# A one-core transformer block: half banks of a set in another order, matmuls of 512 columns in pieces with 8 products, outputs of the plain part issued by SyncE

## The chip, the core and the metric

The kernel runs on one core of a Trainium2 chip. The core has TensorE (PE, matrix products into PSUM), VectorE (DVE), ScalarE (ACT), GpSimd (POOL) and SyncE (SP, which here only issues transfers). The metric is the time of the device for one execution in microseconds; less is better. The engines run side by side, each through its own list of instructions in order, and wait for each other on semaphores.

## The reference

One residual block in float32: model width 2048, sequence 512, batch 1.

```python
hn = rmsnorm(h, norm_mix_g)
proj = hn @ w_in + b_in                       # 2048 x 10248
(q, k, v, o_pre, i_pre, f_pre, cb, cc, ch, gm_pre, gc_pre) = jnp.split(proj, offs, axis=-1)
hm = mlstm_chunkwise(...)                     # 4 heads, chunks of 64
y_m = (head_norm(hm) * jax.nn.sigmoid(o_pre)) @ w_branch_m
y_c = (cb * causal_dwconv(cc * ch, conv_w)) @ w_branch_c
merged = jax.nn.sigmoid(gm_pre) * y_m + jax.nn.sigmoid(gc_pre) * y_c
h = h + merged @ w_out
hn = rmsnorm(h, norm_ffn_g)
u = causal_dwconv(hn @ w_up, ffn_conv_w, ffn_conv_b)   # 2 x 5504 channels
gate, val = jnp.split(u, 2, axis=-1)
h = h + (jax.nn.silu(gate) * val) @ w_down
return rmsnorm(h, norm_out_g)
```

Nearly all the arithmetic is in the dense products with w_in, w_branch, w_out, w_up and w_down.

## The kernel before

Activations lie with channels on the 128 partitions and the 512 time steps along the free axis. The dense products are done by a scheme of the Strassen and Winograd kind: a 2 x 2 arrangement of blocks takes 7 block products and some sums of weights and of activations instead of 8 products. Each float32 factor is split into a high and a low part, and each product is the sum of three matmuls: high weights by high activations (L281), high weights by low activations (L282), low weights by high activations (L283). The helper `three` issues these three.

**Items, pieces, halves.** An item makes two pairs of output blocks. It runs through `nq` pieces of its contraction, each of two halves; `cell_mm` issues one half. An ordinary half has 7 products, so 21 matmuls of 256 columns. One piece of some items (`it.eight`) does the plain 8 products, without the sums of weights (`eight_task`); its halves have 24 matmuls of 256 columns. There are 24 such pieces. Their high weights come from ScalarE at L186 and L187, the others' at L233.

**PSUM.** There are 8 banks of 512 float32 columns, each a tile of its own. Items use two sets in turn: set 0 is banks 0, 1, 2, set 1 is banks 4, 5, 6. A set has six half banks of 256 columns. `PRODUCTS` says which weights and activations go into which bank and half. Bank 3 (`P_BANK`) takes the first product of both sets, a half each; bank 7 (`SIDE`) serves norms and the mLSTM part.

**Evacuation.** After the last half of an item, ScalarE copies the product in bank 3 (`evac_first`, L305), and VectorE adds the banks up in four instructions (`evac_ops`, L311 to L314): L311 reads the first bank of the set, L312 and L313 the second, L314 the third. They stand on VectorE among the sums of weights (L218, L223) and the low weights of the next piece (L237, or L191 and L192 in eight pieces). The low weights have three buffers; PE waits for them at L283, and VectorE waits at L237 for a buffer that PE has freed.

**Plain part.** The last rows of w_down are done without the scheme. There are 16 blocks, `lasts`, of 18 matmuls each (`last_mm`, L1202 to L1204), numbered n = 0 to 15; n below 8 is the first half of the time steps. Block n goes into bank 0, 1, 2 or 4 by n mod 4 (`LBANKS`). Then follow, one step of the program later, the sum with the residual on VectorE (`last_post`, L1215), its square on ScalarE (L1216) and the sum of squares on VectorE (`last_acc`, L1220). After block 9 a matmul with a constant matrix (`last_sum`, L1225, into bank 5; for the second half bank 6) gives the mean over the channels of the first half; `last_root` makes the reciprocal root of it (L1232 on ScalarE, for which a table has to be loaded, then L1233 to L1235 on VectorE). `last_scale` multiplies a block by that and issues its output (L1254). Some blocks have been multiplied by the gain on ScalarE ahead of that (`last_gain`, L1241) and need one instruction on VectorE (L1248); the others need two (L1252).

**Order and waits.** The order of instructions on each engine is the order in which the program issues them, written out by hand in the loop over steps, with a credit for VectorE's time that decides when the stores and sums behind an item (`posts`) go out. Waits are put in for each tile by what was last written or read in it: an instruction that touches a tile waits for the last other engine's access to the tile as a whole.

These lines decide what the change touches:

```python
PRODUCTS = [(1, 0, 0, 0), (6, 4, 0, 1), (5, 3, 1, 0), (4, 2, 1, 1), (2, 1, 2, 0), (3, 6, 2, 1)]
bank = [psum.tile([P, T], F32, tag=f"bank{i}", name=f"bank{i}") for i in range(8)]
P_BANK, SIDE = bank[3], bank[7]
SETS = (bank[0:3], bank[4:7])
LBANKS = (bank[0], bank[1], bank[2], bank[4])
LCOLS = (bank[5], bank[6])
```

## Time and profile before

| | us |
|---|---|
| median of 3 runs | 2601.21 |
| lowest and highest of them | 2599.85, 2602.29 |
| the profiled execution | 2603.19 |
| its span | 2601.5 |

The profiled execution is 1.98 us above the median. Its span is what the rows of the trace are measured in: it starts with the first instruction and ends with the last, and 1.7 us lie outside of it. The main part, items and pieces, runs to 2545.7 us, the plain part from there to the end. PE is busy for 98% of the span, and the granted clock of PE is full in nearly all of the 40 slices; VectorE is busy for 82%, ScalarE for 51%, GpSimd for 33%. A row of a timeline has the start, the duration, the engine, the line, what is written and read (by tile name), partitions and columns, and in brackets how long the engine idled before it and what ended that. Matmul rows overlap: one of 256 columns lasts 0.28 us from issue to end, while the next starts 0.12 us after it. So the pitch of starts is what counts for a stream.

### The profile page before, as it was taken

The page shows a single profiled execution, that of the slowest core. Times are in us where ns is not written, and L with a number is a line of the kernel's source. Part 1 is how long each engine was busy: PE and PEld are TensorE (multiplying, and loading weights), DVE is VectorE, ACT ScalarE, POOL GpSimd, SP SyncE. Part 2 cuts the span into 40 slices and gives each one's busy share as a digit, 9 for nine tenths or more (in the row PEclk, how much of TensorE's full clock was granted, in tenths as well). Part 3 has the DMA queues.
Part 4 walks back from the last instruction along what each step waited for, and adds up shares of the span by engine and source line. Part 5 has one row for each costly group of instructions (what it writes and reads, how often), then busy time and mean ns, then how long its engine had stood idle before and what let it go on. Part 6 is the DMA issues. An engine that isn't in the chain of part 4 may idle for free.

```text
span 2601.5 us, 55134 instructions
## 1 busy us (share of the span) xinstructions
PE 2548.2 (98%) x20886; PEld 2528.9 (97%) x20886; DVE 2123.1 (82%) x3239; ACT 1316.3 (51%) x1731; POOL 862.5 (33%) x996
## 2 busy tenths in 40 slices
PE   9999999999999999999899999999999999999997
PEld 8999999999999999999899999999999999999997
DVE  8687778886777888967889888888888898879766
ACT  7454554546556544445554544454444554545444
POOL 3343333333333212232333333333333323353430
PEclk9999999999999999999999999999999999999998
DMA  9799889898998899999989988898989889999995
GB/s 256 176 238 241 234 225 253 221 256 217 231 253 221 233 297 235 267 271 245 234 220 227 224 224 218 222 224 223 223 221 224 223 223 234 249 273 252 270 228 169
DMA packets 479003, 609.83 MB, mean 234 GB/s; under 512 B 44640, under 2 KB 309856, under 8 KB 478736
## 3 DMA queue, kind: packets, MB, share of 16 engines
q1 hardware_dynamic: 307280, 423.46, 51.5%
q0 software_dynamic: 144224, 137.67, 35.2%
q10 hardware_dynamic: 27232, 45.17, 4.8%
q8 instruction: 163, 2.67, 0.4%
q14 instruction: 104, 0.85, 0.1%
HBM read 541.65 MB, written 60.82 MB: 232 GB/s over the span
## 4 chain that ended last, share of the span: by engine, by line
PE 65%; DVE 5%; DMA 3%; issue 2%; ACT 0%; POOL 0%; DVEq 0%; SPq 0%; ACTq 0%; POOLq 0%
PE bank L283 21%; PE bank L282 21%; PE bank L281 21%; DVE act L361 1%; DVE wl L237 1%; DMA raw<-in_w_out_dram 1%; DMA raw<-in_w_up_dram 1%; DVE raw L218 0%; DMA xraw<-mc_d 0%; DMA xraw<-a_d 0%; DVE xraw L344 0%; PE bank L639 0%; DMA mc_d<-z 0%; PE bank L1204 0%; PE bank L1203 0%
## 5 line engine op out<-in xcount | busy, mean ns | idle before, releaser
L283 PE MATMUL bank<-act,wl 128*128 128x256 f32 x6712 | 1906.1, 284 | 24.3 <-DVE wl L237 23.7
L281 PE MATMUL bank<-act,wh 128*128 128x256 f32 x6712 | 1914.0, 285 | 4.9 <-ACT z L305 2.1
L282 PE MATMUL bank<-act,wh 128*128 128x256 f32 x6712 | 1903.2, 284 | 2.1 <-DVE act L361 2.1
L233 ACT ACTIVATE wh<-raw 128x896 fp32r<-128x896 f32 x904 | 858.2, 953 | 1076.1 <-PE bank L282 719.0
L283 PEld LDWEIGHTS bank<-act,wl 128*128 128x128 f32 x6712 | 1292.2, 193 | 29.2 <-DVE wl L237 29.1
L281 PEld LDWEIGHTS bank<-act,wh 128*128 128x128 f32 x6712 | 1292.2, 193 | 8.5 <-DVE z L311 2.4
L282 PEld LDWEIGHTS bank<-act,wh 128*128 128x128 f32 x6712 | 1292.2, 193 | 5.4 <-DVE act L361 2.5
L237 DVE TENSOR_TENSOR wl<-raw,wh 128x896 fp32r<-128x896 f32 x904 | 982.7, 1088 | 372.2 <-PE bank L283 244.2
L255 POOL DMA_DIRECT2D raw<-in_w_up_dram x344 | 299.2, 952 | 578.7 <-DMA raw<-in_w_up_dram 243.8
L255 POOL DMA_DIRECT2D raw<-in_w_dram x284 | 247.1, 944 | 505.2 <-DMA raw<-in_w_dram 320.9
L255 POOL DMA_DIRECT2D raw<-in_w_down_dram x160 | 141.5, 1002 | 253.0 <-DMA raw<-in_w_down_dram 144.2
L218 DVE TENSOR_TENSOR raw<-raw 128x256 f32<-128x256 f32 x452 | 189.8, 420 | 11.4 <-DMA raw<-in_w_up_dram 5.1
L223 DVE TENSOR_TENSOR raw<-raw 128x256 f32<-128x256 f32 x452 | 189.6, 420 | 0.3
L358 ACT ACTIVATE act<-xraw 128x1792 fp32r<-128x1792 f32 (+1 forms) x52 | 86.9, 1672 | 63.1 <-DVE xraw L354 61.1
L361 DVE TENSOR_TENSOR act<-xraw,act 128x1792 fp32r<-128x1792 f32 (+1 forms) x52 | 103.4, 1988 | 0.0
L688 DVE TENSOR_TENSOR z<-z,rstd 128x1024 f32<-128x1024 f32 x83 | 101.1, 1219 | 0.0
L311 DVE TENSOR_TENSOR z<-bank,z 128x512 f32<-128x512 f32 x122 | 83.6, 685 | 16.2 <-ACT z L305 12.6
L312 DVE TENSOR_TENSOR z<-bank,z 128x512 f32<-128x512 f32 x122 | 83.5, 684 | 0.8
L314 DVE TENSOR_TENSOR z<-bank,z 128x512 f32<-128x512 f32 x122 | 83.4, 684 | 0.0
L255 POOL DMA_DIRECT2D raw<-in_w_out_dram x48 | 42.9, 1019 | 105.3 <-DMA raw<-in_w_out_dram 41.2
L255 POOL DMA_DIRECT2D raw<-in_w_v_dram x32 | 38.6, 1360 | 52.1 <-DMA raw<-in_w_v_dram 32.8
L313 DVE TENSOR_TENSOR z<-bank,z 128x256 f32<-128x256 f32 x122 | 51.8, 424 | 4.2
(247 smaller groups left out, 1302.5 us busy)
## 6 DMA issues: line engine op xcount, KB each, us to landing
raw<-in_w_up_dram SPq DMA_DIRECT2D x172, 512.0 KB, 5.8
raw<-in_w_dram SPq DMA_DIRECT2D x144, 512.0 KB, 6.0
raw<-in_w_up_dram SPq DMA_DIRECT2D x344, 128.0 KB, 4.0
raw<-in_w_up_dram POOLq DMA_DIRECT2D x344, 128.0 KB, 5.5
raw<-in_w_down_dram SPq DMA_DIRECT2D x80, 512.0 KB, 6.6
raw<-in_w_dram SPq DMA_DIRECT2D x284, 128.0 KB, 4.2
raw<-in_w_dram POOLq DMA_DIRECT2D x284, 128.0 KB, 5.3
raw<-in_w_down_dram SPq DMA_DIRECT2D x160, 128.0 KB, 4.5
```

Of the source, the lines that this page charges most:

```text
L218: V.tensor_add(x[:, 6], x[:, 5], x[:, 0])
L223: V.tensor_add(x[:, 2], x[:, 6], x[:, 1])
L233: A.activation(seven(t.wh[r]), half(r), AF.Copy)
L237: V.tensor_sub(seven(t.wl[r]), half(r), seven(f(t.wh[r])))
L255: G.dma_start(at(i), a21, accum_op=ALU.add)
L281: PE.matmul(ps, h, xh, start=start, stop=False, skip_group_check=True)
L282: PE.matmul(ps, h, xl, start=False, stop=False, skip_group_check=True)
L283: PE.matmul(ps, l, xh, start=False, stop=stop, skip_group_check=True)
L311: return [lambda: V.tensor_add(z[:, 0:4:3], b0, two(z[:, 1])), lambda: V.tensor_add(z[:, 1:3], b1, two(z[:, 3])), lambda: V.tensor_add(z[: ...
L358: A.activation(t.act[:, :m], t.raw[:, :m], AF.Copy)
L361: V.tensor_sub(t.act[:, NW:NW + m], t.raw[:, :m], f(t.act[:, :m]))
L688: V.tensor_mul(sb_pair(it.z), sb_pair(it.z), two(rstd))
```

## The change

The three banks of a set become one PSUM tile of 1536 columns, and the six half banks get new products, so that in a piece with 8 products the two half banks that share weights lie side by side and their activations can be read with one stride. Two `three`s of 512 columns replace four of 256. The evacuation reads the same products at their new places. `bank` stays as a list of views of the set tiles, so that the gates and the plain part use the same columns as before, but as parts of the set tiles. In the plain part, outputs are issued by SyncE instead of ScalarE; the gain is multiplied ahead for blocks 1, 3, 5 and 8 to 15, at other places than before, instead of blocks 4 to 15; and one small activation, issued in the step of block 6, uses the table of the root. Lines behind the middle of the file move by one: L1215 is L1216 afterwards, L314 is L315.

```diff
@@ -38,7 +38,7 @@
 K_LAST = 40
 
 
-PRODUCTS = [(1, 0, 0, 0), (6, 4, 0, 1), (5, 3, 1, 0), (4, 2, 1, 1), (2, 1, 2, 0), (3, 6, 2, 1)]
+PRODUCTS = [(1, 0, 0), (6, 4, 2), (5, 3, 3), (4, 2, 4), (2, 1, 1), (3, 6, 5)]
 P1 = (0, 5)
 
 
@@ -120,9 +120,9 @@
     def fwc(which, j): return col(152 + 2 * NF * which, j)
     def fw_neg(which, j): return pneg[:, 24 + NF * which + j:24 + NF * which + j + 1]
 
-    bank = [psum.tile([P, T], F32, tag=f"bank{i}", name=f"bank{i}") for i in range(8)]
-    P_BANK, SIDE = bank[3], bank[7]
-    SETS = (bank[0:3], bank[4:7])
+    SETS = [psum.tile([P, 3 * T], F32, tag=f"set{i}", name=f"set{i}") for i in range(2)]
+    P_BANK, SIDE = (psum.tile([P, T], F32, tag=s, name=s) for s in ("pbank", "side"))
+    bank = [SETS[i // 4][:, i % 4 * T:(i % 4 + 1) * T] if i % 4 < 3 else (P_BANK, SIDE)[i // 4] for i in range(8)]
 
     mA, mB, mC = C([P, 1280], F32, "mA"), C([P, 1032], F32, "mB"), C([P, T], F32, "mC")
     z2 = C([P, 2 * T], F32, "z2")
@@ -277,16 +277,17 @@
 
         def three(ps, ws, xs, start, stop=last):
             h, l = (w[r][:, ws * P:(ws + 1) * P] for w in (t.wh, t.wl))
-            xh, xl = (x[:, b + xs * SW:b + xs * SW + SW] for b in (0, NW))
+            xh, xl = (x[:, b:b + NW].rearrange("p (s n) -> p s n", n=SW)[:, xs] for b in (0, NW))
             PE.matmul(ps, h, xh, start=start, stop=False, skip_group_check=True)
             PE.matmul(ps, h, xl, start=False, stop=False, skip_group_check=True)
             PE.matmul(ps, l, xh, start=False, stop=stop, skip_group_check=True)
 
         if q == it.eight:
             assert not first
+            halves_ = slots(SETS[it.set])
             for k in range(2):
-                for ws, xs, b, half in ((k, 2 * k, 0, 0), (k, 2 * k + 1, 2, 0), (2 + k, 2 * k + 1, 1, 1), (2 + k, 4 + k, 2, 1)):
-                    three(SETS[it.set][b][:, half * H2:(half + 1) * H2], ws, xs, False, last and k == 1)
+                three(halves_[:, 0:2], k, slice(2 * k, 2 * k + 2), False, last and k == 1)
+                three(halves_[:, 4:6], 2 + k, slice(2 * k + 1, 5 + k, 3 - k), False, last and k == 1)
             t.wh[r] = t.wl[r] = None
             return
 
@@ -295,8 +296,8 @@
 
         if last:
             p1()
-        for ws, xs, b, half in PRODUCTS:
-            three(SETS[it.set][b][:, half * H2:(half + 1) * H2], ws, xs, first and half == 0)
+        for ws, xs, i in PRODUCTS:
+            three(slots(SETS[it.set])[:, i], ws, xs, first and i in (0, 2, 4))
         if not last:
             p1()
         t.wh[r] = t.wl[r] = None
@@ -307,11 +308,11 @@
     def evac_ops(it):
 
         z = slots(it.z)
-        b0, b1, b2 = (slots(b) for b in SETS[it.set])
-        return [lambda: V.tensor_add(z[:, 0:4:3], b0, two(z[:, 1])),
-                lambda: V.tensor_add(z[:, 1:3], b1, two(z[:, 3])),
-                lambda: V.tensor_add(z[:, 3], b1[:, 0], z[:, 2]),
-                lambda: V.tensor_add(z[:, 1:3], b2, z[:, 1:3])]
+        b = slots(SETS[it.set])
+        return [lambda: V.tensor_add(z[:, 0:4:3], b[:, 0:4:2], two(z[:, 1])),
+                lambda: V.tensor_add(z[:, 1:3], b[:, 3:5], two(z[:, 3])),
+                lambda: V.tensor_add(z[:, 3], b[:, 3], z[:, 2]),
+                lambda: V.tensor_add(z[:, 1:3], b[:, 1:6:4], z[:, 1:3])]
 
 
     def cell_task(xs, c, d, scale=None, key=None, eight=False):
@@ -464,7 +465,7 @@
 
     combos = [(cs, ct) for cs in range(4) for ct in range(cs, 4)]
     ccol, ecol = C([P, 12, 4], F32, "ccol"), C([P, 4, 4], F32, "ecol")
-    GATE, GATE1 = SETS[1][2], SETS[1][1][:, :H2]
+    GATE, GATE1 = bank[6], bank[5][:, :H2]
     gb = [mA[:, :T], mA[:, T:2 * T], mB[:, :T], mB[:, T:2 * T], mC, z2[:, :T], z2[:, T:]]
 
     gst = mC[:, :KD * 8].rearrange("p (k n) -> p k n", n=8)
@@ -1251,7 +1252,7 @@
                 s = h[:, b * H2:(b + 1) * H2]
                 V.scalar_tensor_tensor(s, s, g_out(j), row, op0=ALU.mult, op1=ALU.mult)
         j1, j2 = kpair(p)
-        A.dma_start(outT[j1:j2 + 1:j2 - j1, :, half * H2:(half + 1) * H2].rearrange("j p t -> p j t"),
+        SP.dma_start(outT[j1:j2 + 1:j2 - j1, :, half * H2:(half + 1) * H2].rearrange("j p t -> p j t"),
                      h.rearrange("p (j t) -> p j t", j=2))
 
 
@@ -1501,11 +1502,10 @@
             for _ in range(2 if it.n < 12 else 1):
                 if finals:
                     last_scale(0, finals.popleft())
-        if not main and it.n > 7:
-            if it.n < 12:
-                last_gain(lasts[it.n - 4])
-            if it.n > 9:
-                last_gain(lasts[it.n - 2])
+        if not main and (it.n in (3, 5, 7) or it.n > 9):
+            last_gain(lasts[it.n - 2])
+        if not main and it.n == 6:
+            A.activation(sm("ny")[:, :1], eps, AF.Abs_reciprocal_sqrt)
     l, = lq
     while lsum:
         last_acc(lsum.pop())
```

**PE, a half of an eight piece.** The rows are the first 12 of 24 matmuls of such a half before (wh and wl are high and low weights, act the activations), and then the first 6 of 12 of the same half afterwards.

```order
L281 MATMUL bank0_80<-act_827_10589,wh_836_10665 128x256 [waits Activation_49]
L282 MATMUL bank0_80<-act_827_10589,wh_836_10665 128x256
L283 MATMUL bank0_80<-act_827_10589,wl_842_10726 128x256 [waits DVE_49]
L281 MATMUL bank2_82<-act_827_10589,wh_836_10665 128x256
L282 MATMUL bank2_82<-act_827_10589,wh_836_10665 128x256
L283 MATMUL bank2_82<-act_827_10589,wl_842_10726 128x256
L281 MATMUL bank1_81<-act_827_10589,wh_836_10665 128x256 [waits Activation_49]
L282 MATMUL bank1_81<-act_827_10589,wh_836_10665 128x256
L283 MATMUL bank1_81<-act_827_10589,wl_842_10726 128x256 [waits DVE_49]
L281 MATMUL bank2_82<-act_827_10589,wh_836_10665 128x256
L282 MATMUL bank2_82<-act_827_10589,wh_836_10665 128x256
L283 MATMUL bank2_82<-act_827_10589,wl_842_10726 128x256
```

```order
L281 MATMUL set0_80<-act_827_10585,wh_836_10661 128x512 [waits Activation_49]
L282 MATMUL set0_80<-act_827_10585,wh_836_10661 128x512
L283 MATMUL set0_80<-act_827_10585,wl_842_10722 128x512 [waits DVE_49]
L281 MATMUL set0_80<-act_827_10585,wh_836_10661 128x512 [waits Activation_49]
L282 MATMUL set0_80<-act_827_10585,wh_836_10661 128x512
L283 MATMUL set0_80<-act_827_10585,wl_842_10722 128x512 [waits DVE_49]
```

Each pair of `three`s that used the same columns of weights has become one with 512 columns, and all write one tile, set0.

**PE, plain part, from block 4 to block 5.** The last three matmuls of block 4 and the first three of block 5, before and then afterwards. act_2472 is the tile of the activations, act_2498 that of the weights, high and low.

```order
L1202 MATMUL bank0_80<-act_2472_30241,act_2498_30574 128x256
L1203 MATMUL bank0_80<-act_2472_30241,act_2498_30574 128x256
L1204 MATMUL bank0_80<-act_2472_30241,act_2498_30574 128x256
L1202 MATMUL bank1_81<-act_2472_30241,act_2498_30574 128x256 [waits Activation_49]
L1203 MATMUL bank1_81<-act_2472_30241,act_2498_30574 128x256
L1204 MATMUL bank1_81<-act_2472_30241,act_2498_30574 128x256 [waits DVE_49]
```

```order
L1203 MATMUL set0_80<-act_2472_29661,act_2498_29994 128x256
L1204 MATMUL set0_80<-act_2472_29661,act_2498_29994 128x256
L1205 MATMUL set0_80<-act_2472_29661,act_2498_29994 128x256
L1203 MATMUL set0_80<-act_2472_29661,act_2498_29994 128x256 [waits DVE_49,Activation_49]
L1204 MATMUL set0_80<-act_2472_29661,act_2498_29994 128x256
L1205 MATMUL set0_80<-act_2472_29661,act_2498_29994 128x256
```

Before, block 5 began in another bank than block 4's, and its first wait was for ScalarE, for the weights. Now it writes the tile that block 4 has written, and its first matmul also waits for VectorE: for the sum L1216 of block 4, which reads that tile.

**ScalarE, plain part, around the first root.** L1216 (L1217 afterwards) is the square of a block, L1241 (L1242) the gain, L1232 (L1233) the root, L1508 the new small activation; hf are the residual tiles. The rows before begin with the gain of block 4 and the square of block 8, those afterwards with the square of block 5.

```order
L1241 ACTIVATE hf_2496_30520<-hf_2496_30520,pcol_71 128x256 [waits Activation_49]
L1241 ACTIVATE hf_2496_30520<-hf_2496_30520,pcol_71 128x256
L1216 ACTIVATE mB_89<-hf_2500_30627 128x512 [waits DMAHW3_49,DVE_49]
L1232 ACT_TABLE_LOAD [waits PE_49]
L1232 ACTIVATE rstd_79<-bank5_85,rs1_106 128x256 [waits Pool_49]
L1241 ACTIVATE hf_2496_30520<-hf_2496_30520,pcol_71 128x256 [waits Activation_49]
L1241 ACTIVATE hf_2496_30520<-hf_2496_30520,pcol_71 128x256
L1216 ACTIVATE mB_89<-hf_2500_30627 128x512 [waits DMAHW4_49,DVE_49]
L1254 DMA out_0_dram<-hf_2496_30520 128x2x256 [waits DVE_49] x2
```

```order
L1217 ACTIVATE mB_85<-hf_2496_29940 128x512 [waits DMAHW0_49,DVE_49]
L1508 ACT_TABLE_LOAD
L1508 ACTIVATE ny_147<-rs1_102 128x1 [waits Pool_49]
L1217 ACTIVATE z1_89<-hf_2496_29940 128x512 [waits DMAHW1_49,DVE_49]
L1242 ACTIVATE hf_2496_29940<-hf_2496_29940,pcol_71 128x256 [waits Activation_49]
L1242 ACTIVATE hf_2496_29940<-hf_2496_29940,pcol_71 128x256
L1217 ACTIVATE z0_88<-hf_2500_30049 128x512 [waits DMAHW2_49,DVE_49]
L1217 ACTIVATE mB_85<-hf_2500_30049 128x512 [waits DMAHW3_49,DVE_49]
L1233 ACTIVATE rstd_79<-set1_81,rs1_102 128x256 [waits PE_49]
L1217 ACTIVATE mB_85<-hf_2500_30049 128x512 [waits DMAHW4_49,DVE_49]
L1242 ACTIVATE hf_2500_30049<-hf_2500_30049,pcol_71 128x256 [waits Activation_49]
```

The load of the table, which before waited for the matmuls of L1225, stands three squares ahead of the root now and waits for nothing. The root itself waits for PE. The outputs have left ScalarE's list.

## The prediction

> **What bounds the kernel now.** I read the page first: busy time, then the chain that ended last, then the groups.

> ```profile
> span 2601.5 us, 55134 instructions
> PE 2548.2 (98%) x20886; PEld 2528.9 (97%) x20886; DVE 2123.1 (82%) x3239; ACT 1316.3 (51%) x1731; POOL 862.5 (33%) x996
> PE 65%; DVE 5%; DMA 3%; issue 2%; ACT 0%; POOL 0%; DVEq 0%; SPq 0%; ACTq 0%; POOLq 0%
> L283 PE MATMUL bank<-act,wl 128*128 128x256 f32 x6712 | 1906.1, 284 | 24.3 <-DVE wl L237 23.7
> L311 DVE TENSOR_TENSOR z<-bank,z 128x512 f32<-128x512 f32 x122 | 83.6, 685 | 16.2 <-ACT z L305 12.6
> ```

> TensorE (PE) is the bound. Its largest group lost 24.3 us waiting, nearly all for VectorE's low weights (L237). So the change can win only where a matmul stream gets shorter on the chain, and loses wherever it makes PE wait. It does both, in different places.

> **The wider matmuls.** One half of an eight piece is 24 matmuls of 256 columns; it becomes 12 of 512. The first two rows below lie exactly one such half apart; the next two stand around three matmuls of 512 columns in the gate work; the last two around 16 of the warm-up's.

> ```profile
> 903.63 0.28 PE L281 MATMUL bank<-act,wh 128*128 128x256 f32 x1
> 906.51 0.28 PE L281 MATMUL bank<-act,wh 128*128 128x256 f32 x1
> ...
> 101.17 0.86 PE L497 MATMUL bank<-act,gw 128*128 128x512 f32 x3
> 101.87 0.28 PE L499 MATMUL bank<-act,gw 128*128 128x256 f32 x1
> ...
> 7.90 3.79 PE L1262 MATMUL bank<-warm 128*128 128x512 f32 x16
> 11.53 0.28 PE L281 MATMUL bank<-act,wh 128*128 128x256 f32 x1
> ```

> 2.88 us for 24 is 0.120 each, so a pair costs 0.240. A wide one takes (101.87 - 101.17) / 3 = 0.233, or in the longer stream (11.53 - 7.90) / 16 = 0.227. The longer stream is the steadier, so I take 13 ns gained per pair; the ends are 7 and 13. There are 24 pieces, 48 halves, 576 pairs. Not all lie where PE sets the end. Each half has one activation at L186 for its high weights. Here are those of three stretches, with the chain's lines in the second and the third:

> ```profile
> L186 ACT ACTIVATE wh<-raw x21: 401/418/420, 896.2 to 998.8; 128x256 fp32r<-128x256 f32 x21
> L186 ACT ACTIVATE wh<-raw x12: 401/418/419, 998.8 to 1057.0; 128x256 fp32r<-128x256 f32 x12
> by line: DMA raw<-in_w_out_dram 26.1%; DMA xraw<-mc_d 10.6%; DVE act L361 10.2%; issue 8.6%; DMA mc_d<-z 7.9%; DVE wl L237 6.9%; DMA mA<-gm_d 6.3%; DVE z L789 2.7%; DMA raw<-in_w_bm_dram 2.5%; DVE xraw L344 2.1%; POOL raw L255 1.7%; DVE raw
> L186 ACT ACTIVATE wh<-raw x13: 417/418/420, 1095.3 to 1220.5; 128x256 fp32r<-128x256 f32 x13
> by line: PE bank L283 33.5%; PE bank L281 33.2%; PE bank L282 33.2%; issue 0.0%
> ```

> The counts share the one at 998.8, and the last one (1220.5) belongs to the four halves behind. So 20 halves up to 998.9 and 12 in 1092.8 to 1220.6 are on a chain that is PE alone; 12 in 998.9 to 1092.8 and 4 after 1220.6 lie where loads and VectorE set the pace, and gain nothing. 32 x 12 x 13 ns = **-5.1 us** (-2.7 at 7 ns; -7.7 if the whole 576 counted at 13).

> [...]

> **Waits on whole sets, main part.** Three banks of a set are now one tile, and a wait is for the tile. Two things follow. First, L311 waited for a matmul with 12 of the half's 21 (9 of 24 in an eight half) still behind it; now it waits for the last, 12 x 0.12 = 1.44 us later at most. Behind it on VectorE stand L312 to L314 and the next L237, for which PE waits.

> ```profile
> DVE wl L237 <- PE bank L283: 244.2, 219, 6.1
> ...
> 1049.93 0.28 PE L281 MATMUL bank<-act,wh 128*128 128x256 f32 x1
> 1051.17 0.39 PE L283 MATMUL bank<-act,wl 128*128 128x256 f32 x1 [0.84 <-DVE wl L237]
> ...
> 1051.03 0.68 DVE L314 TENSOR_TENSOR z<-bank,z 128x512 f32<-128x512 f32 x1
> ```

> The cover is the first row: L237 itself idles 244.2 us, in 219 places, for PE to free a buffer of low weights, so VectorE is usually ahead and a delay of 1.44 us falls into that idle time. Where VectorE is behind, L311 starts after the half's end and loses nothing. I take 0 for it; if the cover were gone, each place would cost up to 1.44.

> Second, an item's first matmul now waits for the last reader of its set (L314 of the item two before), not only for the first. In the example the item starts at 1049.93 and would wait until 1051.03 + 0.68 = 1051.71, about 0.06 more for the signal; its third matmul, which started at 1051.17, would come at 1051.77 + 0.24 = 1052.01: 0.84 us late. There are 30 items that start into a set in this way. I count about ten starts with VectorE that far behind, all in stretches where it sets the pace: what PE loses at the start it mostly would lose at the next L237. I take **+0.9 us**, one such start not given back; ends 0 and ten of them, 8.4.

> **The plain part.** Its 16 blocks of 18 matmuls used four separate banks: block n waited for the sum (L1215) of block n - 4. Now n mod 4 = 0, 1, 2 write into one tile, set 0. Blocks 1, 5, 9, 13 and 2, 6, 10, 14 wait for the sum of the block just before; 3, 7, 11, 15 (set 1) wait for nothing new; block 0 waits for the whole evacuation of the last item.

> ```profile
> 2545.73 0.28 PE L283 MATMUL bank<-act,wl 128*128 128x256 f32 x1
> 2545.85 0.28 PE L1202 MATMUL bank<-act,act 128*128 128x256 f32 x1
> ...
> 2544.68 0.69 DVE L311 TENSOR_TENSOR mA<-bank,mA 128x512 f32<-128x512 f32 x1 [1.63 <-PE bank L283]
> 2547.41 0.68 DVE L314 TENSOR_TENSOR mA<-bank,mA 128x512 f32<-128x512 f32 x1
> ...
> 2567.44 1.03 PE L1225 MATMUL bank<-mC,identw 128*128 128x256 f32 x4
> 2568.12 0.47 PE L1202 MATMUL bank<-act,act 128*128 128x256 f32 x1
> ...
> 2568.55 1.28 ACT L1232 ACT_TABLE_LOAD   x1 [1.08 <-PE bank L1225]
> 2571.62 0.68 DVE L1215 TENSOR_TENSOR hf<-bank,hf 128x512 f32<-128x512 f32 x1
> ...
> 2584.70 0.63 ACT L1216 ACTIVATE z<-hf 128x512 f32<-128x512 f32 x1
> 2585.36 0.69 DVE L1220 TENSOR_TENSOR mB<-mB,z 128x512 f32<-128x512 f32 x1
> 2586.11 2.08 PE L1225 MATMUL bank<-mB,identw 128*128 128x256 f32 x4 [4.69 <-DVE mB L1220]
> 2587.99 2.07 PE L1225 MATMUL bank<-z,identw 128*128 128x256 f32 x4
> 2590.11 0.47 ACT L1232 ACTIVATE rstd<-bank,rs 128x256 f32<-128x256 f32 x1 [1.23 <-PE bank L1225]
> 2590.61 0.43 DVE L1233 SCALAR_TENSOR_TENSOR z<-bank,rstd 128x256 f32<-128x256 f32 x1 [3.96 <-ACT rstd L1232]
> 2591.99 4.91 DVE L1248 TENSOR_TENSOR hf<-hf,rstd 128x512 f32<-128x512 f32 x8
> 2592.72 5.00 ACTq L1254 DMA_DIRECT2D out_dram<-hf  x8
> ```

> - Block 0. L311 comes 1.44 later, so L314 ends at 2547.41 + 0.68 + 1.44 = 2549.53; the block starts at 2549.6 instead of 2545.85: **+3.75**.
> - Blocks 1, 2, 5, 6, 9. From the last matmul's start: 0.28 to its end, 0.1 to VectorE, 0.68 for L1215, 0.06 back, 1.12; the next would have come after 0.12. So 1.0 each: **+5.0**. The sums for block 10 (L1225) then start at 2576.2, and their end, 2568.47 before, is 2577.2.
> - Block 10. It waits for L1215 of block 9, which stands on VectorE behind the root of the first half: sums' end to that L1215 was 2571.62 - 2568.47 = 3.15. The table load goes to the step of block 6, where ScalarE idles, so 1.30 falls off: 1.85 + 0.68 + 0.06 = 2.59, and block 10 starts at 2579.8. It started at 2568.12; 8.75 of the 11.7 are from above, **+2.9** here.
> - To the end. Blocks of 18 x 0.12 = 2.16: 11 at 2582.0, 12 at 2584.1, 13 at 2587.3 and 14 at 2590.4 (1.0 of waiting each), 15 at 2592.6, ended by 2594.8. Block 14's sum, square and L1220 (0.7 each with their gaps, from 2593.0) allow L1225 at 2595.2; 0.9 for four, to 2596.1. Block 15's L1215 now waits for these too (they write its tile), and then comes its square: 2597.6. Four L1225: 2598.5. Root as in the rows (2590.11 to 2591.99 = 1.88): the scaling starts at 2600.4 instead of 2591.99, **+8.4** for the whole part. Some of the 11.7 is given back because PE had finished 4.7 us before the last L1225, and because these took 3.96 us at a cold clock and 1.8 here, where PE has just been busy.

> The eight scalings and outputs behind are as before, issued by SyncE; ScalarE's issues (8 in 5.0 us) only kept pace with L1248's 4.91. Output issues that leave ScalarE in blocks 10 to 15 free some 0.4 us each, already beside the waits above; one more unscaled pair on VectorE (1.0 more) can delay a sum: 0 to +2, I take 0.

> **The clock.** Two of these stalls are long. After such ones the rows show what follows:

> ```profile
> 1270.79 0.58 PE L283 MATMUL bank<-act,wl 128*128 128x256 f32 x1 [2.13 <-DVE wl L237]
> 1270.80:1274.20 3.40, 3.40 (x16) 3.40 (x17) 2.11 (x4) 3.37 (x5) 0.59 (x1) 0.50 1.15 220
> ...
> 2129.98 0.38 PE L283 MATMUL bank<-act,wl 128*128 128x256 f32 x1 [1.57 <-DVE wl L237]
> 2130.40:2133.80 3.40, 3.40 (x31) 3.40 (x30) 3.33 (x7) 0.72 (x1) 0.00 (x0) 1.00 0.91 188
> ```

> A wait of 2.13 us was followed by 3.4 us at clock 0.50 and 16 matmuls where 28 fit (3.40 / 0.12): 1.5 us lost. After 1.57 the clock stayed at 1.00. Blocks 0 and 10 wait 3.6 and 2.8, so I add 2 x 1.5 = **+3.0** (ends 0 and 3.0); the stalls of 1.0 add nothing.

> [...]

> **Sum.** -5.1 + 0.9 + 8.4 + 3.0 = +7.2. The profiled execution took 2603.19, of which 2601.5 is the span; it stands 1.98 above the runs' median of 2601.21. So it would become 2610.4, and the median **2608.4**.

> **Rivals.**
> - *Wide matmuls gain far more* (the other side). Place: the 384 pairs on the chain. It decides from the point where they return the 12.3 us that the rest costs: 32 ns per pair, a pitch of 0.208. Were a wide one as short as a narrow one (0.120), the time would be 2601.2 + 12.3 - 46.1 = 2567. Against it: 0.227 in a stream with nothing else on PE. Chance 0.04. [...]
> - *The plain part hurts less.* No half clock after its stalls and 7.7 from the matmuls: +8.4 - 7.7 + 0.9 = +1.6, 2602.8; with only one of the two, about 2605. For it: 12 of the halves off the chain may shorten a wait after all. Against: waits of 2 us were followed by the cold clock wherever I looked. Chance 0.22.
> - *Late starts tip into the cold clock.* Waits of 1.4 to 1.7 us, as the one at 2129.98, become 2.2 or more, each with 1.5 us at half clock; three of them, or VectorE's extra work in the last blocks, give +4: 2612.5. Chance 0.16.
> - *The change doesn't do what it says*: a wide matmul takes as long as two narrow ones. Then +12.3: 2613.5. Against: both rows of 512 columns. Chance 0.06.

> **How the numbers follow.** The forecast, 2606 to 2611, has 0.50, and 0.02 is left for what I don't see. The range reaches from the second rival (2602) to 2615 (the third rival at the pitch of 0.233 is 2614.9). A measurement of this kernel can tell about 0.2%, 5.2 us, from no change. Slower by more, over 2606.4: 0.47 of the forecast's 0.50, 0.16, 0.06 and 0.01, 0.70. Within: 0.03 and 0.21, 0.25 with the rest. Faster: 0.04 and 0.01 of the second, 0.05.

> **What would show it.** Pitch of matmuls in an eight half, 0.227. Block 0's first matmul (L1203 then) with about 3.6 us idle before it, released by VectorE's L315; blocks 1, 2, 5, 6, 9, 13, 14 with 0.85 to 1.0 released by L1216; block 10 with nearly 3. Clock 0.50 behind the two long ones. The stretch from the last main matmul to the end, 55.8 us now, becomes about 67; everything ahead of it 4 us shorter. It is wrong if PE has no waits on L1216, or if the main part got longer.

## The result and the profile after

The changed kernel takes 2611.78 us (median of 6 runs, 2609.09 to 2616.3), against 2600.39 for the kernel before (6 runs, 2599.7 to 2602.29): 11.4 us more. The ratio is 1.0041, with an interval of 1.0031 to 1.0051, so 8 to 13 us. The predicted median was 2608.4, 7.2 more than before; the measured one lies 0.8 above the likeliest band, 2606 to 2611, and inside the range of 2602 to 2615. The profiled execution has a span of 2608.8 us, 7.3 more than that of before.

The page of the changed kernel gives span, busy times and the engines' shares of the chain that ended last:

```profile
span 2608.8 us, 53743 instructions
...
PE 2543.8 (98%) x20310; PEld 2500.6 (96%) x20310; DVE 2122.5 (81%) x3240; ACT 1316.4 (50%) x1730; POOL 864.5 (33%) x996
...
PE 89%; DVE 6%; DMA 2%; issue 2%; ACT 1%; DVEq 0%; SPq 0%; POOL 0%; ACTq 0%; POOLq 0%
```

PE has 576 matmuls fewer and is busy 4.4 us less, yet the span is longer. So PE's idle time has grown. Two parts have to be told apart: the main part, to the last matmul of L283, and the plain part behind it. Their border and the first of the last eight scalings are these rows of the timeline:

```profile
2542.18 0.28 PE L283 MATMUL set<-act,wl 128*128 128x256 f32 x1
...
2599.31 4.90 DVE L1249 TENSOR_TENSOR hf<-hf,rstd 128x512 f32<-128x512 f32 x8
```

Before, they stood at 2545.73 and 2591.99. The main part ends 3.55 us sooner. The plain part up to the scaling takes 57.13 instead of 46.26, 10.9 more. The view of waits, for PE, says who made it wait (total, times, longest):

```profile
PE set L281 <- DVE z L315: 14.8, 10, 3.3
PE set L1203 <- DVE hf L1216: 8.7, 8, 2.5
PE set L283 <- DVE wl L237: 7.0, 6, 2.1
PE set L281 <- ACT xraw L336: 4.1, 1, 4.1
PE set L1203 <- DVE mA L315: 3.5, 1, 3.5
```

The 24.3 us of L283 are down to 7.0. In their place stand waits of L281, an item's first matmul, for L315, the last reader of its set. The second and the last row are the plain part: eight blocks wait for the sum of the block ahead, and block 0 for the evacuation of the last item.

### The profile page after: what moved, and what is told of

Same layout as the page of the kernel before. It is cut to its first block, busy times and chain, and to the rows that moved or that the text cites. A ratio compares the mean times of both kernels' runs of the same rounds, so it can differ in the third digit from the quotient of the medians.

```text
span 2608.8 us, 53743 instructions
## 1 busy us (share of the span) xinstructions
PE 2543.8 (98%) x20310; PEld 2500.6 (96%) x20310; DVE 2122.5 (81%) x3240; ACT 1316.4 (50%) x1730; POOL 864.5 (33%) x996
## 3 DMA queue, kind: packets, MB, share of 16 engines
q8 instruction: 158, 2.59, 0.4%
## 4 chain that ended last, share of the span: by engine, by line
PE 89%; DVE 6%; DMA 2%; issue 2%; ACT 1%; DVEq 0%; SPq 0%; POOL 0%; ACTq 0%; POOLq 0%
PE set L281 25%; PE set L283 25%; PE set L282 25%; PE pbank L281 4%; PE pbank L282 4%; PE pbank L283 4%; DVE act L362 1%; DVE wl L237 1%; PE side L640 1%; DMA raw<-in_w_out_dram 1%; PE side L442 1%; DMA raw<-in_w_dram 0%; PE set L1203 0%; DMA raw<-in_w_v_dram 0%; DVE raw L218 0%
## 5 line engine op out<-in xcount | busy, mean ns | idle before, releaser
L281 PE MATMUL set<-act,wh 128*128 128x256 f32 (+1 forms) x5616 | 1627.7, 290 | 23.6 <-DVE z L315 14.8
L283 PE MATMUL set<-act,wl 128*128 128x256 f32 (+1 forms) x5616 | 1617.0, 288 | 7.2 <-DVE wl L237 7.0
L282 PE MATMUL set<-act,wh 128*128 128x256 f32 (+1 forms) x5616 | 1616.0, 288 | 1.8 <-DVE act L362 1.8
L237 DVE TENSOR_TENSOR wl<-raw,wh 128x896 fp32r<-128x896 f32 x904 | 981.9, 1087 | 336.0 <-PE pbank L283 209.5
L281 PEld LDWEIGHTS set<-act,wh 128*128 128x128 f32 x5616 | 1082.0, 193 | 37.4 <-DVE z L315 15.5
L283 PEld LDWEIGHTS set<-act,wl 128*128 128x128 f32 x5616 | 1081.8, 193 | 17.2 <-DVE wl L237 8.8
L282 PEld LDWEIGHTS set<-act,wh 128*128 128x128 f32 x5616 | 1082.1, 193 | 12.3 <-DVE act L362 2.0
L255 POOL DMA_DIRECT2D raw<-in_w_up_dram x344 | 298.9, 954 | 579.1 <-DMA raw<-in_w_up_dram 285.2
L255 POOL DMA_DIRECT2D raw<-in_w_dram x284 | 247.3, 949 | 501.9 <-DMA raw<-in_w_dram 299.8
L281 PE MATMUL pbank<-act,wh 128*128 128x256 f32 x904 | 256.8, 284 | 1.6 <-ACT z L306 1.6
L282 PE MATMUL pbank<-act,wh 128*128 128x256 f32 x904 | 256.6, 284 | 0.0
L283 PE MATMUL pbank<-act,wl 128*128 128x256 f32 x904 | 256.5, 284 | 0.0
L255 POOL DMA_DIRECT2D raw<-in_w_down_dram x160 | 141.0, 980 | 251.3 <-DMA raw<-in_w_down_dram 147.8
L218 DVE TENSOR_TENSOR raw<-raw 128x256 f32<-128x256 f32 x452 | 189.5, 419 | 13.5 <-DMA raw<-in_w_out_dram 6.9
L281 PEld LDWEIGHTS pbank<-act,wh 128*128 128x128 f32 x904 | 174.3, 193 | 1.8 <-ACT z L306 1.8
L282 PEld LDWEIGHTS pbank<-act,wh 128*128 128x128 f32 x904 | 174.2, 193 | 0.1
L283 PEld LDWEIGHTS pbank<-act,wl 128*128 128x128 f32 x904 | 174.1, 193 | 0.0
L312 DVE TENSOR_TENSOR z<-set,z 128x512 f32<-128x512 f32 x122 | 83.8, 687 | 46.2 <-issue 20.8
```

Source lines behind the costliest of these rows:

```text
L218: V.tensor_add(x[:, 6], x[:, 5], x[:, 0])
L237: V.tensor_sub(seven(t.wl[r]), half(r), seven(f(t.wh[r])))
L255: G.dma_start(at(i), a21, accum_op=ALU.add)
L281: PE.matmul(ps, h, xh, start=start, stop=False, skip_group_check=True)
L282: PE.matmul(ps, h, xl, start=False, stop=False, skip_group_check=True)
L283: PE.matmul(ps, l, xh, start=False, stop=stop, skip_group_check=True)
```

## The experiments

Each median, in us, is of 5 to 12 executions. The ratio compares with the kernel before on the same chip, whose median was 2600.39 for the first row, 2600.93 for own_tiles to keep_warm, 2600.75 for block0_side to sp_out and 2600.68 for the rest.

| kernel | median | ratio to before, interval |
|---|---|---|
| the changed kernel | 2611.78 | 1.0041 (1.0031 to 1.0051) |
| own_tiles | 2598.36 | 0.9986 (0.9978 to 0.9995) |
| narrow_own | 2600.92 | 1.0003 (0.9994 to 1.0011) |
| plain_only | 2598.4 | 0.9991 (0.9982 to 1.0) |
| keep_warm | 2612.57 | 1.0043 (1.0031 to 1.0056) |
| block0_side | 2608.5 | 1.0031 (1.0022 to 1.004) |
| root_later | 2610.41 | 1.0039 (1.0026 to 1.0051) |
| own_p1_first | 2605.59 | 1.0019 (1.001 to 1.0028) |
| sp_out | 2601.17 | 1.0001 (0.9992 to 1.001) |
| own_evac_ahead | 2602.01 | 1.0009 (1.0 to 1.0017) |
| own_tiles_2 | 2597.68 | 0.9986 (0.9977 to 0.9995) |
| narrow_own_2 | 2601.78 | 1.0002 (0.9993 to 1.001) |
| plain_only_2 | 2597.14 | 0.9986 (0.9977 to 0.9994) |

Single executions differ by more than the terms that were asked for (those of the changed kernel by 7.2 us), and the first 300 us of a profile scatter: the start of "main" below lies at about 297.3 us in own_tiles and 300.1 in narrow_own. So each profile is cut in two lengths as well. "Main" runs from the start of the same two matmuls of 512 columns in all kernels (L598 in before, L599 or L601 in the others; 298.80 in before, 299.57 in the changed kernel) to the last main matmul. "Plain" runs from there to the start of the last eight scalings.

| kernel | main | plain |
|---|---|---|
| before | 2246.9 | 46.3 |
| sp_out | 2245.8 | 45.0 |
| plain_only, plain_only_2 | 2245.4, 2245.6 | 43.2, 43.2 |
| narrow_own, narrow_own_2 | 2248.9, 2248.6 | 44.0, 44.2 |
| own_tiles, own_tiles_2 | 2243.3, 2241.4 | 43.6, 44.0 |
| the changed kernel | 2242.6 | 57.1 |
| keep_warm | 2247.1 | 55.8 |
| block0_side | 2242.0 | 53.9 |
| root_later | 2243.3 | 59.0 |
| own_p1_first | 2249.1 | 44.1 |
| own_evac_ahead | 2250.9 | 44.8 |

**own_tiles: the plain part's blocks back in four tiles of their own.**

```diff
-    LBANKS = (bank[0], bank[1], bank[2], bank[4])
+    LBANKS = (SIDE, bank[4], P_BANK, bank[0])
```

> The changed kernel, but the blocks of the plain part go by n mod 4 into side, the first bank of set 1, pbank and the first bank of set 0: four tiles of their own again. Theory (the plain part's waits on a whole set cost 11.4 us, the wide matmuls win some 5 in the main part): no block of the plain part waits for VectorE, the stretch from the last main matmul to the first scaling falls from 57.1 us to 46 or less, the time is 2594 to 2598, faster than both kernels. Rival (the main part's waits on whole sets eat the gain of the wide matmuls): 2600 to 2604, no better than before.

The theory held for the plain part. Plain fell from 57.1 to 43.6 us and the time to 2598.36, below both kernels. Whether the main part wins anything is for the kernels below to say. In the timeline, block 0 follows the last main matmul without a gap:

```profile
2540.59 0.28 PE L283 MATMUL set<-act,wl 128*128 128x256 f32 x1
2540.71 0.28 PE L1203 MATMUL side<-act,act 128*128 128x256 f32 x1
```

So the plain part's waits on whole sets cost 13.5 us by the profiles (13.2 against own_tiles_2), and 1.0041 less 0.9986 of 2600, some 14 us, by the runs.

**narrow_own: own_tiles with matmuls of 256 columns.**

```diff
-                three(halves_[:, 0:2], k, slice(2 * k, 2 * k + 2), False, last and k == 1)
-                three(halves_[:, 4:6], 2 + k, slice(2 * k + 1, 5 + k, 3 - k), False, last and k == 1)
+                for i in range(2):
+                    three(halves_[:, i], k, 2 * k + i, False, last and k == 1)
+                for i in range(2):
+                    three(halves_[:, 4 + i], 2 + k, (2 * k + 1, 4 + k)[i], False, last and k == 1)
```

> As own_tiles, and the pieces with 8 products use 24 matmuls of 256 columns again, into the same half banks of the set tiles. Theory: the wide matmuls are worth 13 ns for each of the 384 pairs on the chain, so this takes 5.1 us more than own_tiles (2.7 to 7.5 as ends). Rival: the stretches behind them take it all back, 0 to 1 us more. Against plain_only it shows what the wait for a whole set costs in the main part: 0 to 2 us by my prediction, 5 or more if it is the main cost.

It took 2.6 us more than own_tiles in the medians, which is the lower end, and 5.6 more in main in the profiles. That left the worth of the wide matmuls open; hence the repetitions below.

**plain_only: the kernel before with the edits of the plain part alone.**

```diff
-        A.dma_start(outT[j1:j2 + 1:j2 - j1, :, half * H2:(half + 1) * H2].rearrange("j p t -> p j t"),
+        SP.dma_start(outT[j1:j2 + 1:j2 - j1, :, half * H2:(half + 1) * H2].rearrange("j p t -> p j t"),
...
-        if not main and it.n > 7:
-            if it.n < 12:
-                last_gain(lasts[it.n - 4])
-            if it.n > 9:
-                last_gain(lasts[it.n - 2])
+        if not main and (it.n in (3, 5, 7) or it.n > 9):
+            last_gain(lasts[it.n - 2])
+        if not main and it.n == 6:
+            A.activation(sm("ny")[:, :1], eps, AF.Abs_reciprocal_sqrt)
```

> The kernel before, with only the edits of the plain part: outputs issued by SyncE, the gain multiplied ahead for other blocks, the table loaded in the step of block 6. Theory: the table load of 1.28 us leaves the chain of the first root, the rest is hidden, so 0.5 to 2 us less than before (2598.5 to 2600). Rival: outputs on SyncE and one more unscaled block on VectorE cost more than that: 2601 to 2602.

It gained 2.5 us, a little more than expected, with an interval that ends at no gain. Its 2598.4 is also the time of own_tiles (2598.36): by these medians all that own_tiles wins over before comes from the edits of the plain part, and merged sets with wide matmuls win nothing in sum. The timeline of ScalarE shows the table load far ahead of the root, which then starts without it:

```profile
2557.54 1.28 ACT L1507 ACT_TABLE_LOAD   x1
...
2565.66 0.47 ACT L1232 ACTIVATE rstd<-bank,rs 128x256 f32<-128x256 f32 x1 [1.66 <-PE bank L1225]
```

**keep_warm: the changed kernel with matmuls that fill block 0's wait.** Their results go into side and nothing reads them.

```diff
         x = plain["x"]
+        if l.n == 0:
+            for _ in range(27):
+                PE.matmul(SIDE[:, :H2], t.wh[:, :P], x[:, :H2], start=True, stop=True, skip_group_check=True)
```

> The changed kernel with 27 matmuls more, of 256 columns, into side ahead of block 0, whose results nothing reads: they fill 3.2 us of the 3.5 that PE idles there, and cost nothing themselves if the wait is set by VectorE. Theory (the idle time puts PE at half clock): the clock stays at 1.00 in the 3.4 us behind and the first scaling comes 1.5 us sooner after the last main matmul, 55.6 instead of 57.1. Rival (the half clock does not come from the idle time, or is hidden): 57.1 as before, or more.

Windows of 3.4 us behind block 0's start, first of the changed kernel and then of this one. The columns are length, busy time and count of PE, of its weight loads, VectorE, ScalarE and GpSimd, then PE's granted clock, the DMA's share and GB/s.

```profile
2545.96:2549.36 3.40, 3.40 (x17) 3.40 (x18) 0.81 (x1) 1.34 (x2) 1.21 (x1) 0.54 1.04 214
```

```profile
2549.36:2552.76 3.40, 2.52 (x19) 2.35 (x20) 1.76 (x3) 1.57 (x3) 1.21 (x1) 1.00 1.10 233
```

The clock is 0.54 behind the idle wait and 1.00 behind the filled one, and plain is 1.4 us shorter (55.8 against 57.1). The theory held to 0.2 us there; the time as a whole, 2612.57, doesn't resolve so little.

**block0_side: only block 0 in a tile of its own.** The sum reads the same `lbank(n)`.

```diff
+    def lbank(n):
+        return LBANKS[n % 4] if n else SIDE
...
-        ps = LBANKS[l.n % 4]
+        ps = lbank(l.n)
```

> The changed kernel, with block 0 alone of the plain part in side instead of set 0. Theory (block 0's wait for the whole evacuation costs 3.7 us and 1.4 at half clock): block 0 starts without a wait, block 1 then waits some 1.5 us for the evacuation instead of 1.0 for block 0's sum, the clock stays at 1.00; the first scaling comes 52.5 us after the last main matmul instead of 57.1, the time falls by 4.6 us to about 2607. Rival (the wait only moves): block 1 waits as long as block 0 did, 57.

It gained 3.3 us by the medians (2.6 by the ratios, whose intervals overlap) and 3.3 in plain, not 4.6. Block 1 waits for the evacuation as expected, and no half clock follows there; the clock is 1.00 from 2542.90 to 2546.30 us:

```profile
2544.66 0.36 PE L1206 MATMUL set<-act,act 128*128 128x256 f32 x1 [1.44 <-DVE mA L315]
```

But block 10's wait, 2.54 us in both kernels, is now followed by half clock, while behind it in the changed kernel the clock was 1.00 (the last section has the rows). The windows of this kernel and of the changed one:

```profile
2572.80:2576.20 3.40, 3.40 (x18) 3.40 (x18) 1.61 (x4) 0.78 (x2) 0.00 (x0) 0.50 0.65 192
```

```profile
2578.10:2581.50 3.40, 3.40 (x28) 3.40 (x29) 2.88 (x6) 1.62 (x4) 0.00 (x0) 1.00 0.50 155
```

So the wait itself is worth what was expected (4.6 less the 1.4 of the clock is 3.2), and the half clock has moved.

**root_later: the first root behind block 9's sum.**

```diff
             last_post(l)
+            if l.n == 9:
+                last_root(0)
             lsum.append(l)
...
         if not main and it.n == 9:
-            last_root(0)
             finals.extend(range(8))
```

> The changed kernel, with the first root issued behind block 9's sum instead of ahead of it. Theory (block 10 waits 2.8 us because that sum stands behind the root on VectorE): block 10's wait falls to 0.3 us or less, the first scaling comes 54.6 us after the last main matmul instead of 57.1, the time falls by 2.5 us to about 2609. Rival (what bounds the end behind block 10 is VectorE's list, not PE): block 10 starts sooner and the scaling does not, 57.

Neither held. Block 10's wait is gone from PE's timeline, where L1226 runs straight into it. But the scalings that follow the root now stand ahead of block 12's sum, and block 13 waits 2.17 us for it. 

```profile
2586.09 0.38 PE L1203 MATMUL set<-act,act 128*128 128x256 f32 x1 [2.17 <-DVE hf L1216]
```

Behind that, 6.8 us run at half clock. The window of the first 3.4 of them:

```profile
2587.50:2590.90 3.40, 2.62 (x13) 2.32 (x12) 1.65 (x4) 0.94 (x3) 0.00 (x0) 0.50 0.22 77
```

Plain is 1.8 us longer in this profile, and the median 1.4 us shorter; the intervals overlap. With the blocks still in one tile, the wait has moved down VectorE's list.

**own_p1_first: an item's first half begins with the product for pbank.**

```diff
-        if last:
+        if first or last:
             p1()
...
-        if not last:
+        if not first and not last:
             p1()
```

> own_tiles, and the first half of an item issues the product that goes into pbank first instead of last. Theory (the main part loses by item starts that wait for the last reader of their set): three matmuls, 0.36 us, run beside each such wait; the eleven waits in stretches that VectorE paces fall by 0.36 each, but about half of that comes back at the next low weights, so 1 to 3 us less than own_tiles. Rival (these stretches are paced by VectorE whatever PE does): the same as own_tiles within 0.5.

The theory fell: 7.2 us more than own_tiles. pbank holds a half for each set, so it is also one tile for both, and the item's first matmul now waits for ScalarE's copy for the item just ended:

```profile
PE pbank L281 <- ACT z L306: 19.8, 16, 4.2
PE set L283 <- DVE wl L237: 5.7, 6, 2.0
```

The wait for L315 was traded for one as long for L306. Eight spells of 3.4 us at half clock fall into main, where own_tiles had 6 and 4.

**sp_out: only the outputs on SyncE** (the first hunk of plain_only).

> The kernel before, with only the outputs issued by SyncE. plain_only as a whole took 2.5 us off. Theory (most of that is the table load and the gains that leave ScalarE in the last blocks): 0 to 0.8 us less than before. Rival (the issues on ScalarE, 0.4 to 0.6 us each beside the squares, were the cost): 1.5 to 2.5 us less.

No difference in time (1.0001), as the theory had it, with plain 1.3 us shorter in one profile. So, as far as medians of this spread show, most of plain_only's gain comes from the other edits, the table and the gains, which were not parted further.

**own_evac_ahead: the last reader of a set ahead of the next low weights on VectorE.**

```diff
-        weave(evs[2:], los)
+        weave(evs[2:])
+        weave(los)
```

> own_tiles, and on VectorE the last evacuation of an item (the last reader of its set) comes ahead of the next piece's first low weights instead of behind them. Theory (the main part loses by item starts that wait for that reader): the ten starts that waited 16.7 us begin some 1.0 us sooner, and PE then waits for the low weights two matmuls later; a wait is cut in two, so fewer reach 2 us and half clock. 1 to 4 us less than own_tiles. Rival (VectorE paces these stretches, the order within it doesn't matter): within 0.5 of own_tiles, or more, since low weights come 0.7 later everywhere else.

The rival held, in its worse form: 4.3 us more than own_tiles_2 on the same chip. The waits, first of this kernel and then of own_tiles:

```profile
PE set L283 <- DVE wl L237: 13.2, 22, 1.9
PE set L281 <- DVE z L315: 11.8, 8, 2.7
```

```profile
PE set L281 <- DVE z L315: 16.7, 10, 3.5
PE set L283 <- DVE wl L237: 5.9, 7, 2.1
```

What L315 gained, the low weights lost, and in more places (22 against 7). The two rows add up to 25.0 us against 22.6, which is not all of the loss. Nine spells of 3.4 us at half clock fall into main, where own_tiles had 6 and 4; at up to 1.5 us each, an estimate from the spell in the prediction's rows, they can be the rest, which isn't shown.

**The repetitions.**

> own_tiles once more, to set it beside narrow_own_2 on one chip: the wide matmuls' worth as the difference. Theory: 4 to 5 us less than narrow_own_2 (the working gave 5.1). Rival: 2.6 or less, as the first medians have it.

> narrow_own once more. Against plain_only_2 on the same chip it gives the cost of the waits on whole sets in the main part: 0.9 us by the prediction's sum; 2.5 to 3 by the first medians; about 6 if all the idle time that PE has more there counts.

> plain_only once more: 2 to 3 us less than before, if the first median (2.5 less) holds; the stretch from the last main matmul to the first scaling 43.2 us again, instead of 46.3.

narrow_own_2 is 4.1 us above own_tiles_2, and 4.6 above plain_only_2, which is 3.5 below before; plain_only_2's plain is 43.2 again. By ratios both pairs of own_tiles and narrow_own say 0.0016 to 0.0017, some 4.3 us, with an uncertainty of about 3.

The main lengths give another split. The four kernels with separate banks have 2245.4 to 2246.9 (mean 2245.9), the two with whole sets and narrow matmuls 2248.9 and 2248.6, the six with whole sets and wide matmuls whose main part is the changed kernel's 2241.4 to 2247.1 (mean 2243.3). By them whole sets cost 2.8 us in the main part and wide matmuls give back 5.5. But each is a single execution, and the profiled ones were not typical: those of own_tiles lie 2.9 and 2.2 us below their medians, those of narrow_own 3.3 and 1.6 above theirs. So 5.5 is likely too much. By the medians whole sets cost 2.5 and 4.6 (narrow_own against plain_only), wide matmuls give back 2.6 and 4.1, and the two together come to 0.0 and +0.5 (own_tiles against plain_only), each with an uncertainty of 2 to 3.

## Why the prediction was right

The direction and the terms of the plain part, which is the large loss, were right. The gain in the main part was forecast too large: 4.2 us, where the profiles show 2.7 and the medians about nothing.

**Wide matmuls, -5.1.** The pitch was right. The timeline of the changed kernel shows the pitch; 24 wide matmuls lie between these two rows:

```profile
905.00 0.40 PE L281 MATMUL set<-act,wh 128*128 128x512 f32 x1
...
910.46 0.39 PE L281 MATMUL set<-act,wh 128*128 128x512 f32 x1
```

5.46 / 24 = 0.2275, as the warm-up's stream had it. What it is worth is less certain: the main lengths give -5.5 and the medians -2.6 and -4.1. Two products in the working are off by a little: 384 x 13 ns is 5.0 us, and 576 x 13 ns is 7.5, not 7.7. The rival of far shorter matmuls does not hold here.

**Waits on whole sets in the main part, +0.9.** This term was mis-sized: 2.8 us by the main lengths, 2.5 and 4.6 by the medians (narrow_own against plain_only). The part costed at nothing, the later L311, did not show as waits for low weights: kernels with whole sets have fewer of these (7.7 to 8.8 us in the two narrow ones, 23.6 to 23.7 in the two of plain_only). The starts of items were the cost. One place, before (first four rows) and after (the last three):

```profile
2254.29 0.69 DVE L311 TENSOR_TENSOR z<-bank,z 128x512 f32<-128x512 f32 x1
...
2255.03 0.39 PE L281 MATMUL bank<-act,wh 128*128 128x256 f32 x1 [0.56 <-DVE z L311]
...
2256.28 1.08 DVE L237 TENSOR_TENSOR wl<-raw,wh 128x896 fp32r<-128x896 f32 x1
...
2257.42 0.58 PE L283 MATMUL bank<-act,wl 128*128 128x256 f32 x1 [1.89 <-DVE wl L237]
```

```profile
2248.50 0.68 DVE L312 TENSOR_TENSOR z<-set,z 128x512 f32<-128x512 f32 x1
...
2251.50 0.68 DVE L315 TENSOR_TENSOR z<-set,z 128x512 f32<-128x512 f32 x1
...
2252.23 0.58 PE L281 MATMUL set<-act,wh 128*128 128x256 f32 x1 [3.31 <-DVE z L315]
```

From the first evacuation's start, PE reached the item's third matmul after 3.13 us before. Now its first comes after 3.73, and the third follows two matmuls behind. That is 0.60 + 0.24 = 0.84 us late, as much as in the prediction's example. The count, ten, was right too (10 waits for L315). Of the ten I let one stand, and 2.8 us are more than three. Two readings are open. Less of what PE loses at a start may be lost anyway at the next low weights than I took. Or the rest is the clock: the kernels with separate banks had 4, 4, 5 and 6 spells of half clock in main, the two with whole sets and narrow matmuls 5 and 7. On average that is 1.25 more, at 1.5 us each up to 1.9 of the 2.8, an estimate from six profiles; then 0.9 would be left for the waits themselves, and the missing term would be that of the third rival, late starts that tip into half clock. No run parts the two.

**The plain part, +8.4 and +3.0.** 10.9 more in the profile, where the sum had 11.4. Block 0 waited 3.50 us, and others as foretold:

```profile
2545.96 0.58 PE L1203 MATMUL set<-act,act 128*128 128x256 f32 x1 [3.50 <-DVE mA L315]
...
2550.62 0.36 PE L1203 MATMUL set<-act,act 128*128 128x256 f32 x1 [0.88 <-DVE hf L1216]
...
2578.10 0.39 PE L1203 MATMUL set<-act,act 128*128 128x256 f32 x1 [2.54 <-DVE hf L1216]
...
2589.09 0.39 PE L1203 MATMUL set<-act,act 128*128 128x256 f32 x1 [0.78 <-DVE hf L1216]
```

Two sizes inside it were off and nearly cancel. The waits with their half clock cost 13.5 us (against own_tiles), where the sum, without the table load's 1.3 that it had taken off, has 8.4 + 1.3 + 3.0 = 12.7; half clock followed block 0's wait only, 1.4 instead of 3.0, so the waits by themselves came to some 12 where the sum had 9.7. That one spell and not two came was a matter of where block 10's wait fell (last section). So the near agreement of the totals is in part luck. And the edits of the plain part are worth 3.0 by themselves (46.3 to 43.2) instead of 1.3. The working also put an unscaled block at 1.0 more on VectorE; the rows of plain_only have 0.87 for one and 0.68 for a scaled one, 0.2 more.

**The sum.** -5.5 + 2.8 + 10.9 = 8.2 from the profiles, against 7.2 predicted. The runs say 11.4, with 8 as the lower end of the interval. The medians point to the main part: there the two terms cancel (own_tiles against plain_only), and the plain part's 10.9 alone is 0.5 from 11.4. That is a likely reading and no more, with these uncertainties, and since executions of the changed kernel spread over 7 us. The time came close to the third rival's 2612.5, but not by its three more spells in main: the changed kernel has 6 there, before has 5.

## What to carry to other kernels

When buffers are merged so that one instruction can span them, the waits merge as well: list every user of the old buffers, those far from the place of the gain too, and look for a first writer that now waits for the last reader. Here wider matmuls that gain 3 to 5 us cost 14 in a tail that used the same banks one by one, and one line that gave the tail other tiles returned it. In the main part the waits on merged tiles took most or all of the gain back.

## What the runs showed of the hardware that I had not expected

```profile
2573.01:2576.42 3.41, 2.55 (x19) 2.10 (x17) 0.32 (x1) 0.47 (x1) 0.00 (x0) 1.00 0.00 0
2576.42:2579.83 3.41, 1.73 (x14) 1.73 (x15) 3.34 (x8) 1.43 (x3) 0.00 (x0) 1.00 0.01 5
```

```profile
2569.41:2572.82 3.41, 0.87 (x6) 0.66 (x6) 2.58 (x7) 1.15 (x3) 0.00 (x0) 1.00 0.00 0
```

In the changed kernel the border at 2576.42 cuts the wait, and PE is idle for 0.86 us of one slice and 1.68 of the next; no half clock follows. In block0_side all 2.54 us lie in one slice, and the next slice runs at half clock. The 14 traces agree. From 298 to 2590 us they have 84 slices at full clock in which PE is idle for 1.82 us or more, and half clock follows each; of the 9201 with 1.70 or less it follows two. Before and the changed kernel by themselves have 13 slices with 1.83 us or more, and half clock follows each, and 1315 with 1.68 or less, and it follows none. What sets the grid, no run shows.

So in these traces the number of spells goes with where the waits fall on the grid. In main, kernels with the same instructions on PE there had 4 (own_tiles_2, 2241.4 us) to 7 (keep_warm, 2247.1). That may be a source of the spread between executions, but not all of it: the two narrow kernels have 5 and 7 spells and nearly the same length, 2248.9 and 2248.6.
